# Three-chunk first task and a position-major last projection in a two-layer encoder

## The chip, the core and the metric

The kernel runs on one core of a Trainium2 chip. The metric is device time in microseconds. In the profile PE is TensorE (PEld its weight loads), DVE is VectorE, ACT is ScalarE, POOL is GpSimd and SP is the queue that issues most DMAs.

## The reference

Two layers of a pre-norm encoder on x of 512 positions and 1024 features, all float32. Each layer projects the normed x once, feeds two attention branches, multiplies each by a SiLU gate, and projects back with a residual add. A norm ends the whole.

```python
for layer in range(DEPTH):                       # DEPTH = 2
    h = rms_norm(x, norm_g[layer])
    p = h @ w_in[layer]                          # 1024 -> 6304
    c_q, c_kv, k_r, gate_a, dil_qkv, gate_b = jnp.split(p, split_points, axis=-1)
    a = mla_attention(c_q, c_kv, k_r, ...) * jax.nn.silu(gate_a)     # 8 heads, low-rank q (384) and kv (256)
    b = dilated_attention(dil_qkv, cos_d, sin_d) * jax.nn.silu(gate_b)  # 3 groups x 8 heads
    x = x + jnp.concatenate([a, b], axis=-1) @ w_out[layer]          # 1024 -> 1024
return rms_norm(x, final_g)
```

## The kernel before, in words

**Precision.** Every operand of a large product is held as two parts, hi and lo. `triple` issues three matmuls per product: hi by hi, hi by lo, lo by hi. Weights come from HBM as tiles of 128 x 512 (`wst`, in the order of `PLAN`). `prefetch` loads a tile into `wraw` (3 buffers), ScalarE converts the hi part (L192) and VectorE subtracts for the lo part (L197); the result lies in `whl` (4 buffers). `weight` asks for tiles three ahead of the one in use. `hl` (14 buffers of hi and lo, 128 x 512) holds the normed input chunks, the latents and the eight chunks that the output projection reads.

**Layout.** Features lie on the partitions and positions along the free axis: x is eight chunks of 128 features x 512 positions. `take_x` multiplies a chunk by the norm's gain and splits it (L270 on ScalarE, L271 on VectorE). The norm's factor per position is applied later, so products start before it is known. `add_square` squares a chunk and adds it to a running sum `L.ss` on GpSimd (L265); `norm` turns the sum to positions with transposes (L250).

**Order.** `Weave` writes the order of the program out ahead of time: a main list of tasks (projections) advances a clock by the cost that each step yields, and side lists (norms, scores, values, combinations) step in where their needs are done and a lag has passed. The instructions of an engine run in the order that results after the compiler's scheduling.

**The start.** Eight x chunks are loaded on SP's queue with the first four weight tiles among them, `take_x` is issued for each and then all squares, the first two of them on GpSimd. The first main task, ("ckv",), is `latent_pair`: for each x chunk, six matmuls into two banks. Then comes ("v", 1, 0), the value projection of 288 columns, and then ("cq", 2), ("cq", 0), ("cq", 1), 24 matmuls each. `keep_latent` stores a result and adds its square (L347, GpSimd).

**The end of a layer.** The output projection has eight blocks n of 128 output features, each a sum over eight chunks `ms`: four from the first branch (`mo`) and four from the second (`do`). `out_part` runs some chunks of one block: tasks "wp" (chunks 0 to 3), "wq" (4 and 5, as soon as do 0 and 1 are there) and "wo" (the rest). Before the last ones the second branch's unit 11 has to be finished: transposes, value products (`far_out`, L766), `combine`, `combine_last`. `out_add` loads the x chunk into `xl` (2 buffers), adds it to the bank (L829), and in layer 0 stores it to `x1d` and hands it to the next layer's `take_x` and `add_square`.

**The end of the kernel.** In layer 1 the blocks 3, 4, 6 and 7 are computed in two halves of 256 positions (`out_halves`), so that `final` can start on the first half. `out_add` squares each result on ScalarE (L832), multiplies it by the final gain (L833) and adds squares on GpSimd (L839). `final` turns the sums (L250), forms the factor with small VectorE instructions (L890 to L899), spreads it by transposes (L904) and multiplies each block (L913 for the first half, L915 for the second) before eight stores.

Of the kernel before, what the change touches and what calls it, by code (L numbers as in the profile page):

```python
# [7 lines left out]
F32 = mybir.dt.float32  # L8
# [6 lines left out]
S = 512  # L15
# [22 lines left out]
def plan():  # L38

    t = []  # L40
    for task in ORDER:
        n = {"v": 8 if task == ("v", 1, 0) else 4, "mv": 1, "muk": 1, "mur": 1, "muq": 1 - task[1] % 2 if len(task) > 1 else 0, "kr": 0}.get(task[0], 2)
        t += [("ckv", c, i) for i in range(2) for c in range(2)] if task[0] == "ckv" else [task + (i,) for i in range(n)]
    t += [("wo", n, 0) for n in range(5)] + [("wo", n, 1) for n in range(3)]
    t += [("wo", n, i) for n, i in ((5, 0), (3, 1), (4, 1), (5, 1), (6, 0), (6, 1), (7, 0), (7, 1))]
    return t
# [3 lines left out]
PLAN = plan()  # L50
ADDED = ("dqk", "nv", "ga", "gb")
FIRST = PLAN.index(("dqk", 0, 1, 1))
# [79 lines left out]
def hybrid_encoder(ctx, tc, xT, wst, gains, tables, keytab, masks, out):  # L132
# [36 lines left out]
    gn = const.tile([128, 2 * NG + 8], F32, name="gn")  # L169
# [14 lines left out]
    def prefetch(upto):  # L184
        while emitted[0] < min(upto, len(queue)):
            l, i = queue[emitted[0]]
            c = WCOLS.get(PLAN[i][0] if PLAN[i][:3] != ("v", 1, 0) else "vk", 512)
            raw = t([128, 512], F32, "wraw", 3)
            nc.sync.dma_start(raw[:, :c], wst[l * len(PLAN) + i, :, :c])
            w = wtile(l, PLAN[i])  # L190
            hi, lo, src = w[:, 0, :c], w[:, 1, :c], raw[:, :c]
            nc.scalar.copy(hi, src)  # L192
            if PLAN[i][0] in ADDED and i > FIRST:
# [4 lines left out]
            ready[(l,) + PLAN[i]] = w  # L198
# [57 lines left out]
    def add_square(L, x, pool=False):  # L256
        q = tmp()
        if pool:
            nc.gpsimd.tensor_tensor(q, x, x, op=ALU.mult)
        else:  # L260
            nc.scalar.activation(q, x, AF.Square)
        if L.ss is None:
            L.ss = q
        else:
            nc.gpsimd.tensor_tensor(L.ss, L.ss, q, op=ALU.add)  # L265
# [16 lines left out]
    Z = Layer()  # L282
    Z.ss, Z.q = None, []

    nc.scalar.activation(ones[:, 1:2], ones[:, 0:1], AF.Exp)
    warm = hl()
# [4 lines left out]
    xs = []  # L291
    for k in range(8):
        x = ogt() if k < 6 else xl()
        nc.sync.dma_start(x, xT[128 * k:128 * k + 128])
        xs.append(x)
        take_x(layers[0], k, x)
        if k in (0, 4):
            prefetch(emitted[0] + 2)
    for k, x in enumerate(xs):
        add_square(layers[0], x, k < 2)  # L300
# [32 lines left out]
    def keep_latent(L, name, c, a):  # L333
# [12 lines left out]
        else:  # L346
            nc.gpsimd.tensor_tensor(L.sq[name], L.sq[name], q, op=ALU.add)  # L347
# [7 lines left out]
    def latent_pair(L):  # L355

        a = [bank(), bank()]
        for i in range(2):
            w = [weight(L.l, "ckv", c, i) for c in range(2)]
            for k in range(4 * i, 4 * i + 4):  # L360
                for c in range(2):
                    quads(a[c], w[c], L.h[k:k + 1], k, 8)
                if k < 7:
                    yield 1.3, 0.0
        for c in range(2):
            keep_latent(L, "ckv", c, a[c])
        yield 1.3, 0.0
# [454 lines left out]
    def out_add(L, n, a, c, last):  # L822

        if n not in L.x:
            x = ogt() if last and n in (3, 4) else xl()
            nc.sync.dma_start(x, (xT if L.l == 0 else x1d)[128 * n:128 * n + 128])
            L.x[n] = (x, ogt() if last and n in (0, 1, 2, 5) else x)
        x, y = L.x[n]
        nc.vector.tensor_tensor(y[:, c], x[:, c], a, op=ALU.add)  # L829
        if last:  # L830
            q = tmp()
            nc.scalar.activation(q[:, c], y[:, c], AF.Square)  # L832
            nc.scalar.mul(y[:, c], y[:, c], gn[:, 2 * NG + n:2 * NG + n + 1])  # L833
            if n == 0:
                Z.ss = q
            elif n > 5:
# [281 lines left out]
```

## Time and profile before

| | |
|---|---|
| median of 3 runs | 949.06 us (949.03 to 950.31) |
| profiled execution | 949.16 us |
| its span | 947.4 us |
| PE busy | 913.3 us (96%) |
| VectorE busy | 698.8 us (74%) |
| ScalarE busy | 599.7 us (63%) |
| GpSimd busy | 342.5 us (36%) |
| HBM read, written | 112.74 MB, 4.36 MB |

A row of the order of time gives start, length, engine, source line, operation, output and input with shapes, count, and in brackets the idle time of the engine ahead of it with what ended it. L235 to L237 are the three matmuls of `triple`. A matmul's length is its latency; what one costs in a stream is the step from one start to the next.

### The profile page before, as it was taken

What the parts mean: (1) busy time and instruction counts of PE and PEld (TensorE: products, weight loads), DVE (VectorE), ACT (ScalarE), POOL (GpSimd) and SP (SyncE); (2) the same over time, 40 slices, a digit from 0 to 9 for tenths busy, and PEclk for the clock granted to TensorE, in tenths of its full rate; (3) what the DMA queues carried; (4) which work ended last, traced back from release to release, by engine and by line L of the source; (5) the groups of instructions that cost most, each with busy time, mean ns of one, the idle gap of its engine ahead of it and who ended that gap; (6) DMA issues with size and microseconds to landing.
All of it is one profiled execution on the core that took longest, in us unless ns stands there. A gap on an engine that the chain in (4) does not pass through costs nothing.

```text
span 947.4 us, 16052 instructions
## 1 busy us (share of the span) xinstructions
PE 913.3 (96%) x5252; PEld 777.3 (82%) x5252; DVE 698.8 (74%) x1730; ACT 599.7 (63%) x1447; POOL 342.5 (36%) x393
## 2 busy tenths in 40 slices
PE   7999999999999999998999999999999989999995
PEld 4978888988889889877897888888888878887874
DVE  7756788967868766787766488797876866857775
ACT  5546786666857766754554578666766666676452
POOL 6125262344632431333211435424554224234223
PEclk9999999999999999999999999999999999999997
DMA  6448443177553764652653754516756455376342
GB/s 228 132 109 170 105 101 87 48 163 157 117 127 90 147 133 101 140 139 90 217 167 97 167 118 91 109 43 144 145 124 136 112 118 111 92 149 142 99 135 90
DMA packets 83123, 118.15 MB, mean 125 GB/s; under 512 B 16800, under 2 KB 31968, under 8 KB 83040
## 3 DMA queue, kind: packets, MB, share of 16 engines
q1 hardware_dynamic: 63456, 81.47, 29.7%
q0 software_dynamic: 19584, 35.66, 23.8%
q8 instruction: 41, 0.67, 0.3%
q14 instruction: 42, 0.34, 0.1%
HBM read 112.74 MB, written 4.36 MB: 124 GB/s over the span
## 4 chain that ended last, share of the span: by engine, by line
PE 78%; DVE 9%; ACT 4%; DMA 3%; issue 3%; POOL 1%; SPq 1%; DVEq 0%; POOLq 0%; ACTq 0%
PE bank L235 22%; PE bank L236 21%; PE bank L237 21%; PE bank L430 4%; PE bank L531 3%; PE bank L725 1%; DMA whl<-wst 1%; PE bank L654 1%; PE bank L766 1%; DVE pt L216 1%; DMA tmp<-shd 1%; DVE whl L197 1%; ACT p L509 1%; DVE tmp L611 1%; ACT whl L192 1%
## 5 line engine op out<-in xcount | busy, mean ns | idle before, releaser
L235 PE MATMUL bank<-hl,whl 128*128 128x512 f32 (+1 forms) x836 | 329.8, 396 | 7.1 <-ACT hl L215 4.8
L237 PE MATMUL bank<-hl,whl 128*128 128x512 f32 (+1 forms) x836 | 324.2, 388 | 5.3 <-DMA whl<-wst 3.4
L236 PE MATMUL bank<-hl,whl 128*128 128x512 f32 (+1 forms) x836 | 325.1, 389 | 1.8 <-DVE hl L271 1.7
L192 ACT CAST whl<-wraw 128x512 fp32r<-128x512 f32 (+2 forms) x256 | 151.5, 597 | 123.7 <-PE bank L237 83.9
L195 POOL DMA_DIRECT2D whl<-wst x136 | 119.8, 890 | 222.9 <-ACT whl L194 154.5
L237 PEld LDWEIGHTS bank<-hl,whl 128*128 128x128 f32 x836 | 157.6, 189 | 40.0 <-DMA whl<-wst 4.2
L235 PEld LDWEIGHTS bank<-hl,whl 128*128 128x128 f32 x836 | 157.4, 189 | 39.3 <-ACT hl L215 6.3
L236 PEld LDWEIGHTS bank<-hl,whl 128*128 128x128 f32 x836 | 158.0, 189 | 31.9 <-DVE hl L271 4.0
L197 DVE TENSOR_TENSOR whl<-wraw,whl 128x512 fp32r<-128x512 f32 (+3 forms) x120 | 87.9, 741 | 37.1 <-ACT whl L192 35.7
L609 POOL TENSOR_TENSOR tmp<-tmp,sd 128x512 f32<-128x512 f32 x48 | 63.1, 1315 | 88.7 <-DVE tmp L607 72.0
L216 DVE TENSOR_TENSOR pt<-bank,pt 128x512 fp32r<-128x512 f32 x128 | 83.6, 683 | 5.4 <-ACT pt L215 4.0
L194 ACT ACTIVATE whl<-wraw 128x512 fp32r<-128x512 f32 x136 | 86.3, 634 | 0.1
L235 PE MATMUL bank<-whl,hl 128*128 128x256 f32 (+1 forms) x288 | 83.1, 290 | 0.0
L236 PE MATMUL bank<-whl,hl 128*128 128x256 f32 (+1 forms) x288 | 82.1, 285 | 0.0
L237 PE MATMUL bank<-whl,hl 128*128 128x256 f32 (+1 forms) x288 | 82.0, 285 | 0.0
L215 ACT CAST pt<-bank 128x512 fp32r<-128x512 f32 x128 | 69.8, 588 | 10.0 <-PE bank L430 9.6
L511 POOL TENSOR_SCALAR p<-p,lc 128x512 f32<-128x512 f32 x64 | 48.7, 768 | 73.6 <-DVE lc L510 72.8
L430 PE MATMUL bank<-ident,p 128*128 128x128 f32 x512 | 67.0, 273 | 0.0
L430 PEld LDWEIGHTS bank<-ident,p 128*128 128x128 f32 x512 | 58.6, 140 | 5.4
L738 ACT ACTIVATE p<-p,st 128x128 f32<-128x128 f32 x128 | 50.0, 393 | 15.1 <-DVE st L734 14.8
L509 ACT ACTIVATE p<-bank,nm 128x512 f32<-128x512 f32 x64 | 43.5, 684 | 23.3 <-DVE nm L506 22.9
L235 PEld LDWEIGHTS bank<-whl,hl 128*128 128x128 f32 x288 | 54.7, 190 | 0.6
(183 smaller groups left out, 1566.6 us busy)
## 6 DMA issues: line engine op xcount, KB each, us to landing
wraw<-wst SPq DMA_DIRECT2D x224, 256.0 KB, 3.1
whl<-wst POOLq DMA_DIRECT2D x136, 256.0 KB, 4.5
tmp<-shd SPq DMA_DIRECT2D x32, 128.0 KB, 3.3
xl<-xT SPq DMA_DIRECT2D x10, 256.0 KB, 2.6
wraw<-wst SPq DMA_DIRECT2D x16, 144.0 KB, 2.9
wraw<-wst SPq DMA_DIRECT2D x12, 192.0 KB, 2.4
x1d<-xl SPq DMA_DIRECT2D x8, 256.0 KB, 2.3
out_dram<-p SPq DMA_DIRECT2D x8, 256.0 KB, 2.1
```

The lines of the kernel that those rows point to most:

```text
L192: nc.scalar.copy(hi, src)
L194: nc.scalar.mul(lo, src, -1.0)
L195: nc.gpsimd.dma_start(lo, wst[l * len(PLAN) + i, :, :c], accum_op=ALU.add)
L197: nc.vector.tensor_tensor(lo, src, F(hi), op=ALU.subtract)
L215: nc.scalar.copy(dst_hi, src)
L216: nc.vector.tensor_tensor(dst_lo, src, F(dst_hi), op=ALU.subtract)
L235: nc.tensor.matmul(a, w[:, 0], h[:, 0], start=first, stop=False)
L236: nc.tensor.matmul(a, w[:, 0], h[:, 1], start=False, stop=False)
L237: nc.tensor.matmul(a, w[:, 1], h[:, 0], start=False, stop=last)
L430: nc.tensor.transpose(b[:, 128 * i:128 * i + 128], x, ident)
L509: nc.scalar.activation(pt, s, AF.Exp, bias=nm[:, qb, a:a + 1], scale=1.0, accum_out=l1)
L609: nc.gpsimd.tensor_tensor(u, u, L.sd, op=ALU.mult)
```

## The change

1. *First task.* In layer 0, ("ckv",) and ("cq", 2) become one task of three chunks (`latent_first`): nine matmuls for each x chunk. Its six weight tiles are loaded into `p` tiles and held in `hl`. The first 128 columns of three tiles are loaded as pieces on ScalarE's DMA queue; the rest comes on SP's queue behind the second x chunk and the fifth.
2. *Squares.* In layer 0 all squares are formed on ScalarE inside the first task and added on VectorE. In both layers the ("ckv") square is added on VectorE.
3. *Layer 0's output.* The tasks "wq" run for five blocks instead of three, and the second-half weight tiles of blocks 0 to 4 lie in `hl`.
4. *Layer 1's output.* Positions lie on the partitions: four blocks sc of 128 positions, two halves of 512 features. The residual block is loaded from `x1d` in a rearranged form, transposed into the bank, and the products are added onto it; weight tiles are 128 x 512 slices of one chunk each. `out_sums` squares the bank with a sum per partition on ScalarE, forms the factor with nine small VectorE instructions, multiplies by factor and gain (a broadcast tile `L.gb`) and stores 128 x 512 pieces. `out_halves`, `final` and the last sums on GpSimd are gone.

```diff
+    one, rest = slice(0, 128), slice(128, 512)
+    raws = [t([128, 512], F32, "p", 8) for _ in range(6)]
...
+    for j in range(3):
+        nc.scalar.dma_start(raws[j][:, one], wst[j, :, one])
...
     for k in range(8):
...
+        load(k)
+        if k == 1:
+            for j in range(3):
+                nc.sync.dma_start(raws[j][:, rest], wst[j, :, rest])
+        elif k == 4:
+            for j in range(3, 6):
+                nc.sync.dma_start(raws[j], wst[j])
+    for j in range(3):
+        take_weights(j, one)
+    for k in range(8):
+        take_x(layers[0], k, xs[k])
+        if k in (1, 4):
+            for j in range(3):
+                take_weights(j if k == 1 else j + 3, rest if k == 1 else slice(0, 512))
...
+    def latent_first(L):
+
+        chunks = FIRST if L.l == 0 else FIRST[:2]
+        a = [bank() for _ in chunks]
         for i in range(2):
-            w = [weight(L.l, "ckv", c, i) for c in range(2)]
+            w = [weight(L.l, *c, i) for c in chunks]
             for k in range(4 * i, 4 * i + 4):
-                for c in range(2):
+                for c in range(len(chunks)):
                     quads(a[c], w[c], L.h[k:k + 1], k, 8)
+                if L.l == 0:
+                    add_square(L, xs[k])
...
-            nc.gpsimd.tensor_tensor(L.ss, L.ss, q, op=ALU.add)
+            (nc.gpsimd if L.l else nc.vector).tensor_tensor(L.ss, L.ss, q, op=ALU.add)
...
-            nc.gpsimd.tensor_tensor(L.sq[name], L.sq[name], q, op=ALU.add)
+            (nc.vector if name == "ckv" else nc.gpsimd).tensor_tensor(L.sq[name], L.sq[name], q, op=ALU.add)
...
-        if l + 1 == DEPTH and key[0] == "wo" and key[1] > 5:
+        if key[0] == "wo" and (key[1] < 6 and key[2] if l + 1 == DEPTH else key[1] < 5 and key[2]):
             return hl()
...
+    def load_x(L):
+
+        sc, half = L.order.pop(0)
+        x = xl()
+        nc.sync.dma_start(x.rearrange("p (n c) -> p n c", n=4),
+                          x1d[512 * half:512 * half + 512, 128 * sc:128 * sc + 128].rearrange("(n p) c -> p n c", p=128))
+        L.x.append(x)
...
+    def out_rows(L, blocks, half, chunks):
 
         ms = L.mo + L.do
...
+        for sc in blocks:
+            if (sc, half) not in L.acc:
+                a, x = bank(), L.x.pop(0)
+                for j in range(4):
+                    nc.tensor.matmul(a[:, 128 * j:128 * j + 128], x[:, 128 * j:128 * j + 128], ident, start=j == 0, stop=False, is_transpose=True)
+                L.acc[sc, half] = a
+                if L.order:
+                    load_x(L)
+                yield 0.44, 0.0
+        for k in chunks:
+            if (k, half) not in L.wo:
+                L.wo[k, half] = weight(L.l, "wo", k, half)
+            for sc in blocks:
+                triple(L.acc[sc, half], ms[k][:, :, 128 * sc:128 * sc + 128], L.wo[k, half], False, k == 7)
+                if k == 7:
+                    out_sums(L, sc, half)
+                yield 0.65, 0.0
+
+    def out_sums(L, sc, half):
...
+        a = L.acc[sc, half]
+        if half == 0:
+            L.o[sc] = [t([128, S], F32, "p", 8) for _ in range(2)], sm(2, "sq%d" % sc)
+        o, ss = L.o[sc]
+        nc.scalar.activation(tmp(), a, AF.Square, accum_out=ss[:, half:half + 1])
+        if half == 0:
+            nc.vector.tensor_tensor(o[0], a, L.gb[:, 0], op=ALU.mult)
+            return
...
+        nc.scalar.mul(o[0], o[0], r)
+        nc.vector.scalar_tensor_tensor(o[1], a, r, L.gb[:, 1], op0=ALU.mult, op1=ALU.mult)
+        for j in (1, 0):
+            nc.sync.dma_start(out[128 * sc:128 * sc + 128, 512 * j:512 * j + 512], o[j])
...
+            task(main, k("wa"), now(*mla), out_rows, (0, 1), 0, range(4))
+            task(main, k("wb"), [], out_rows, (2,), 0, range(4))
+            task(main, k("wc"), now(k("s", "d", 11)), out_rows, (3,), 0, range(4))
+            task(main, k("wd"), [], out_rows, (0,), 1, range(4))
+            task(main, k("we"), now(*early), out_rows, range(4), 0, (4, 5))
+            task(main, k("wf"), [], out_rows, (0,), 1, (4, 5))
+            task(main, k("wg"), now(k("o", "d", 11)), out_rows, (1,), 1, range(6))
+            task(main, k("wh"), now(*late), out_rows, range(4), 0, (6, 7))
+            task(main, k("wi"), [], out_rows, (0, 1), 1, (6, 7))
+            for sc in (2, 3):
+                task(main, k("wj", sc), [], out_rows, (sc,), 1, range(8))
+            continue
...
-        for n in range(3):
+        for n in range(5):
             task(main, k("wq", n), now(*early), out_part, n, range(4, 6))
```

More of the change, by code (lines that the diff above doesn't have):

```diff
@@ L129, in run, with hybrid_encoder @@
                 return
-def hybrid_encoder(ctx, tc, xT, wst, gains, tables, keytab, masks, out):
+def hybrid_encoder(ctx, tc, xT, wst, gains, fgain, tables, keytab, masks, out):
     nc = tc.nc
@@ L820, in combine_last, with out_add @@
         yield 0.0, 0.5
[L822 to L836, printed above, removed]
-                Z.q.append(q[:, c])
-            else:
-                nc.gpsimd.tensor_tensor(Z.ss[:, c], Z.ss[:, c], q[:, c], op=ALU.add)
-            return
-        nc.sync.dma_start(x1d[128 * n:128 * n + 128], y)
-        take_x(layers[L.l + 1], n, y)
-        add_square(layers[L.l + 1], y)
+    def out_add(L, n, a):
+        x = xl()
+        nc.sync.dma_start(x, xT[128 * n:128 * n + 128])
+        nc.vector.tensor_tensor(x, x, a, op=ALU.add)
+        nc.sync.dma_start(x1d[128 * n:128 * n + 128], x)
+        take_x(layers[L.l + 1], n, x)
+        add_square(layers[L.l + 1], x)
     def out_part(L, n, chunks):
@@ L894, in final @@
         nc.vector.tensor_scalar(h, m, -0.5, 0.0, op0=ALU.mult, op1=ALU.add)
         for _ in range(3):
-            for i in range(2):
-                yi = y[:, i:i + 1]
-                nc.vector.scalar_tensor_tensor(z[:, i:i + 1], yi, yi, h[:, i:i + 1], op0=ALU.mult, op1=ALU.mult)
-            nc.vector.scalar_tensor_tensor(y, z, 1.5, y, op0=ALU.add, op1=ALU.mult)
-        rst = y
-        yield 0.6, 2.5
-        b = bank()[:, 0:256]
-        for i in range(2):
-            nc.tensor.transpose(b[:, 128 * i:128 * i + 128], rst[:, i:i + 1].to_broadcast([128, 128]), ident)
@@ L985, in hybrid_encoder @@
         last = l + 1 == DEPTH
+        if last:
+            at = [i for i, x in enumerate(main) if x[0] == k("gb", 2)][0]
+            line = []
+            task(line, k("ahead"), now(k("mur", 1)), load_ahead)
+            main[at:at] = line
+            task(main, k("wa"), now(*mla), out_rows, (0, 1), 0, range(4))
[9 more added lines that the diff above has]
+                task(main, k("wj", sc), [], out_rows, (sc,), 1, range(8))
+            continue
@@ L986, in hybrid_encoder @@
         for n in range(3):
             task(main, k("wp", n), now(*mla), out_part, n, range(4))
-        if last:
-            task(main, k("wp", 3), now(k("s", "d", 11)), out_halves, (3, 4), range(4), range(2))
-        else:
-            for n in (3, 4):
-                task(main, k("wp", n), now(k("s", "d", 11)), out_part, n, range(4))
-        for n in range(3):
+        for n in (3, 4):
+            task(main, k("wp", n), now(k("s", "d", 11)), out_part, n, range(4))
+        for n in range(5):
@@ L1115 @@
     out = np.empty((S, D), np.float32)
-    out[order()] = r.results[0]["out_0_dram"].T
+    out[order()] = r.results[0]["out_0_dram"]
     return out[None]
```

156 lines of the change are left out of this document (61 added, 95 removed).

## The prediction, on record before the result

> **What bounds the kernel now.** I read the page first, then the busy time by stretches, then the order of time at both ends and at the two output projections.
>
> ```profile
> span 947.4 us, 16052 instructions
> PE 913.3 (96%) x5252; PEld 777.3 (82%) x5252; DVE 698.8 (74%) x1730; ACT 599.7 (63%) x1447; POOL 342.5 (36%) x393
> PE 78%; DVE 9%; ACT 4%; DMA 3%; issue 3%; POOL 1%; SPq 1%; DVEq 0%; POOLq 0%; ACTq 0%
> ```
>
> TensorE is busy for 96% of the span and is 78% of the chain that ended last. So a change pays where TensorE stands still, or where its work disappears. The stretches (length, busy time of PE, weight loads, VectorE, ScalarE, GpSimd, then granted clock, DMA share, GB/s) show where it stands:
>
> ```profile
> 15.00:20.00 5.00, 2.14 (x7) 1.18 (x7) 5.00 (x4) 1.60 (x4) 4.76 (x4) 0.97 0.34 88
> 20.00:25.00 5.00, 5.00 (x17) 3.91 (x16) 2.24 (x3) 0.31 (x1) 0.66 (x1) 0.69 0.51 161
> 38.90:56.00 17.10, 17.10 (x81) 14.17 (x80) 12.37 (x34) 8.85 (x20) 2.79 (x5) 1.00 0.32 96
> 880.00:890.00 10.00, 8.71 (x39) 6.71 (x38) 9.28 (x28) 5.33 (x17) 4.19 (x6) 1.00 0.21 60
> 900.00:910.00 10.00, 8.41 (x43) 6.59 (x42) 9.42 (x18) 3.17 (x7) 1.64 (x1) 1.00 0.19 58
> 910.00:920.00 10.00, 9.47 (x55) 7.99 (x54) 7.13 (x10) 7.54 (x13) 2.59 (x2) 1.00 0.55 162
> 935.00:948.00 13.00, 1.57 (x9) 0.73 (x7) 7.36 (x26) 0.93 (x2) 3.36 (x5) 0.61 0.47 161
> ```
>
> From 15 to 20 us VectorE is full (5.00 of 5.00) and TensorE at 2.14; then the granted clock drops to 0.69. In the last 13 us TensorE has 1.57 us of work. Between these ends little is lost.
>
> **The start, part by part.** Three things change: the columns for chunk 0 come first as small pieces through ScalarE's queue; the running sum of squares leaves GpSimd; and the first task takes ("cq", 2) along, so each x chunk feeds nine matmuls instead of six.
>
> ```profile
> 4.04 0.72 ACT L270 ACTIVATE hl<-og,gn 128x512 fp32r<-128x512 f32 x1 [1.80 <-DMA og<-xT]
> 4.72 0.62 ACT L192 CAST whl<-wraw 128x512 fp32r<-128x512 f32 x1
> 4.79 0.82 DVE L271 SCALAR_TENSOR_TENSOR hl<-og,gn,hl 128x512 fp32r<-128x512 f32 x1 [3.35 <-ACT hl L270]
> 5.53 0.68 DVE L197 TENSOR_TENSOR whl<-wraw,whl 128x512 fp32r<-128x512 f32 x1
> 8.10 6.38 DVE L271 SCALAR_TENSOR_TENSOR hl<-og,gn,hl 128x512 fp32r<-128x512 f32 x4 [0.17 <-ACT hl L270]
> 8.90 5.02 POOL L265 TENSOR_TENSOR tmp<-tmp,tmp 128x512 f32<-128x512 f32 x3
> 25.17 0.55 PE L235 MATMUL bank<-whl,hl 128*128 128x288 f32 x3
> 38.69 0.60 PE L250 MATMUL bank<-ident,tmp 128*128 128x128 f32 x4
> 39.04 0.47 PE L235 MATMUL bank<-hl,whl 128*128 128x512 f32 x1
> 39.35 0.39 PE L236 MATMUL bank<-hl,whl 128*128 128x512 f32 x1
> 45.74 0.39 PE L237 MATMUL bank<-hl,whl 128*128 128x512 f32 x1
> 59.79 0.66 PE L250 MATMUL bank<-ident,tmp 128*128 128x128 f32 x4 [0.95 <-POOL tmp L347]
> GB/s 0 0 23 161 391 259 199 303 328 344 393 404 404 385 385 386 383 400 373 188 18 0 23 174 0 193 309 358 36 35 251 154 106 0 0 0 201 266 230 55
> wraw<-wst SPq DMA_DIRECT2D x4, 256.0 KB, 5.8
> ```
>
> *Why VectorE is late now.* The residual-part instruction of take_x took 0.82 us at 4.79 and 6.38/4 = 1.60 us each while GpSimd added squares beside it. With those seven adds on VectorE nothing runs on GpSimd there; they cost 7 x 0.68 = 4.8 us of VectorE, but stand behind all take_x work in order.
>
> *TensorE's need.* From 39.35 to 45.74 lie 28 steps of a 512-wide matmul: 6.39/28 = 0.228 us. The first task becomes 72 x 0.228 = 16.4 us, and the 24 matmuls of ("cq", 2), 24 x 0.228 = 5.5 us, vanish behind the value task. So today the equivalent point is 25.17 + 5.5 = 30.7 us.
>
> *When it is fed.* The throughput row (40 slices of 0.75 us over the first 30 us) adds up to 0.47 MB (gains, three 64 KB pieces, the first x) at about 4.0 us; with half a microsecond to land, 4.5. ScalarE now also issues three DMAs ahead of its table load, but its first conversion is at 4.04 today. 0.72 of ScalarE and 0.82 of VectorE give the second half at 6.1, and eight more matmuls end chunk 0 at 8.0. The rest of the three pieces (1.32 MB in all) is through at 7.2 and landed near 8, just in time; its conversions are 3 x 0.5 on ScalarE and 3 x 0.55 on VectorE (from 0.62 and 0.68, scaled for 384 columns). The last x (3.7 MB in all) lands near 14, and its VectorE part is done by 16, while TensorE comes to it at 8.0 + 6 x 2.05 = 20.3. So from chunk 1 TensorE is the limit: 8.0 + 63 x 0.228 = 22.4, and 0.5 for hand-overs: 22.9 us instead of 30.7, **-7.8 us**. Bounds: as early as now (5.4 + 16.4 = 21.8) gives -8.9; the same 25.17 as now gives -5.5. I take the inner value because it is counted from rows of this very stretch.
>
> *Is it kept?* The six weight tiles sit in hl and p, so whl and wraw are free for the value task's first weights. SP's queue has the same x loads and tables; the fourth weight no longer waits there for a free raw buffer. In the 17.10 us of the three cq chunks VectorE works 12.37; without ("cq", 2) TensorE has 11.6 us there and VectorE 12.37 - 2 x 0.68 - 0.82 = 10.2. It still fits, narrowly. The ("ckv") add on VectorE costs and gains nothing: the wait for L347 at 59.79 is for the cq sum, which stays on GpSimd.
>
> **Layer 0's output.** Chunks 4 and 5 of n = 3, 4 move ahead of the second half of unit 11, with the second-half weights in hl instead of the four whl.
>
> ```profile
> PE bank L235 <- ACT hl L215: 1.3, 1, 1.3
> PE bank L766 <- DVE pt L216: 0.2, 1, 0.2
> L829 DVE TENSOR_TENSOR xl<-xl,bank x8: 676/686/691, 451.5 to 477.6; 128x512 f32<-128x512 f32 x8
> 479.07 0.75 DVE L271 SCALAR_TENSOR_TENSOR hl<-xl,gn,hl 128x512 fp32r<-128x512 f32 x1 [0.79 <-ACT hl L270]
> 480.37 0.39 PE L235 MATMUL bank<-hl,whl 128*128 128x512 f32 x1
> ```
>
> The waits of 440 to 450 us are 1.5 us; 12 x 0.228 = 2.7 us of moved work covers them. But the last value products of unit 11 then stand about 0.9 us later, and the eight residual adds (two xl buffers, 26.1 us from first to last) start from there. Today the last chunk is ready at 479.82, 0.55 us before its use; that slack goes and most of the 1.5 is waited again: **-0.4**, between -1.5 and +1.5.
>
> **The last projection.** Same products: 4 position blocks x 2 halves x 8 chunks x 3 = 192 of 512 columns; today 96 of these are pairs of 256.
>
> ```profile
> 919.44 0.28 PE L235 MATMUL bank<-hl,hl 128*128 128x256 f32 x1
> 925.08 0.28 PE L237 MATMUL bank<-hl,hl 128*128 128x256 f32 x1
> xl<-xT SPq DMA_DIRECT2D x10, 256.0 KB, 2.6
> tmp<-shd SPq DMA_DIRECT2D x32, 128.0 KB, 3.3
> ```
>
> 47 steps in 5.64 us: 0.12 for 256 columns, so full width saves 96 x (0.24 - 0.228) = 1.1 us. New are 32 transposes that put the residual into PSUM; four took 0.35 (38.69 to 39.04): +2.8. The 8 transposes of the first half's final norm go: -0.7. In the planner's order 27 matmuls (6 today) now stand between unit 11's transposes and its value products, and a transposed block with 18 (12 today) between these and the late chunks; there TensorE idles 1.59 + 0.53 = 2.1 us from 900 to 920: -2.1. Sum **-1.1**; if the idle time stays and the halves cost nothing, +2.1; if the transposes also fill the 1.3 us idle of 880 to 890, -2.4. VectorE loses eight residual adds and gains four multiplications and 36 tiny ones, ScalarE loses eight gain products and gains four, GpSimd is freed: all beside 40 us of matmuls. A new wait stands in SP's queue: the third residual block waits for a transpose to free one of two buffers, with weight loads behind it; these run three tiles ahead. The gain's 512 KB load waits for the rope tile's last reader, long done.
>
> **The tail.** Now: last matmul at 934.75, end at 947.4, 12.65 us.
>
> ```profile
> 934.75 0.29 PE L237 MATMUL bank<-hl,hl 128*128 128x256 f32 x1
> 938.87 0.16 DVE L899 SCALAR_TENSOR_TENSOR sfy<-sfz,sfy 128x2 f32<-128x2 f32 x1
> 940.02 0.16 DVE L899 SCALAR_TENSOR_TENSOR sfy<-sfz,sfy 128x2 f32<-128x2 f32 x1
> 943.02 0.74 DVE L915 TENSOR_TENSOR p<-xl,bank 128x256 f32<-128x256 f32 x2
> out_dram<-p SPq DMA_DIRECT2D x8, 256.0 KB, 2.1
> L509 ACT ACTIVATE p<-bank,nm 128x512 f32<-128x512 f32 x64 | 43.5, 684 | 23.3 <-DVE nm L506 22.9
> 878.09 0.19 ACT L738 ACTIVATION_READ_ACCUMULATOR p<-p,st 128x1 f32 x1
> ```
>
> After: matmul and hand-over 0.34; square with sum, like the exponential from PSUM, 0.68 + 0.19; hand-over 0.1; nine tiny VectorE instructions at 1.15/6 = 0.19 (six steps lie between 938.87 and 940.02) = 1.73; the product out of PSUM 0.82, with ScalarE's 0.72 beside it; then what now follows the last VectorE instruction (943.76 to 947.4), 3.64, and 0.4 as two stores come together: 7.9 with a hand-over. **-4.7**; -5.2 without the second store, -3.5 if two stores take turns and each hand-over costs 0.3 more.
>
> **Sum.** -7.8 - 0.4 - 1.1 - 4.7 = -14.0: span 933.4. The profiled execution took 949.16, 1.76 beyond its span, and the median of the runs is 949.06, so the forecast is 935.2 us, 14.0 under the profiled execution and 13.9 under the median. All bounds together: -18.0 to -5.4.
>
> **Rivals.**
> (a) *The clock drops at the new start too.* For it: the clock fell after a stretch in which TensorE was busy 2.14 of 5 us. Against: there is less idle time now between 5 and 8 us. Price: 0.31 of 5 us, 1.6; 936.8. Chance 0.10. The Trainium skill, "TensorE: Matmul & The Clock Gate", What's actually happening, has the clock fall after a whole idle window of some 3.4 us and warm again after one busy window. By that rule the new start keeps full clock and the sum stays; the trace does not quite agree, since its fall came with 2.14 us of matmuls in the five before.
> (b) *VectorE takes over behind the value task.* 10.2 us of partly dependent work in 11.6: if it needs its old pace for half of the removed 5.5, 2.7 come back: 937.9. Chance 0.14.
> (c) *More is filled*: chunk 0 as early as now (-1.1), layer 0's wait gone (-1.1), transposes free in 880 to 890 (-1.3): 931.7. Chance 0.13.
> (d) *Slower: the residual loads bind.* A block is now 512 rows of 512 bytes. With two buffers a load is hidden while it lands within about 6 us (two blocks of 12 x 0.228 + 0.35); to lose 14.0 over six further loads, each must cost 2.3 more of TensorE's time, landing after some 11 us: 950. A 256 KB load lands in 2.6, and 128 KB in such short rows in 3.3; twice that is 6.6. Chance 0.04.
> (e) *The shorter ends do not matter*, the time staying within 0.2%: the chain passes through both ends, so only 0.02.
>
> **Numbers.** The forecast itself has 0.57, with its own range 932.3 to 938.2. (a) and (b) are slower, (c) faster, and all but (d) and (e) are well below 949; 0.2% (1.9 us) is about what a measurement tells from no change. Range 930.5 to 941.2: it leaves out (d), (e) and the far corners. Faster 0.94, same 0.02, slower 0.04.
>
> **What would show it.** The 288-column matmuls begin near 22.9 us, with the VectorE part of take_x at 0.8 us each; granted clock 1.0 from 15 to 25; the three latent chunks' end 7.8 us earlier; no wait on hl between the two halves of unit 11; 32 transposes at 0.09 us; under 8 us between the last matmul and the end. Wrong it would be by a late start of the value task, a wait of TensorE for x's last chunk at the layer boundary, or weight casts that stall ahead of the last projection.

## The result and the profile after

The changed kernel takes 933.06 us, the median of four runs (932.15 to 936.2); before, 949.04 (946.65 to 950.31). The ratio is 0.984 (95% interval 0.981 to 0.9871): shorter by 16 us, 1.6 per cent. The forecast was 935.2 with a range of 930.5 to 941.2. The profiled execution is the longest of the four: 936.2 us, of which the span is 934.4, 13.0 below the span before.

Of the page, the same three lines as before:

```profile
span 934.4 us, 15835 instructions
PE 910.4 (97%) x5172; PEld 775.1 (83%) x5172; DVE 690.9 (74%) x1732; ACT 597.8 (64%) x1448; POOL 315.1 (34%) x367
PE 81%; DVE 8%; ACT 4%; DMA 3%; issue 3%; POOL 1%; ACTq 0%; DVEq 0%; POOLq 0%
```

TensorE has 2.9 us less busy time, and the span is 13.0 shorter: most of the gain is time in which it stood still. The busy time by stretches (columns as before: PE, weight loads, VectorE, ScalarE, GpSimd, granted clock, DMA share, GB/s):

```profile
15.00:20.00 5.00, 5.00 (x24) 4.14 (x23) 4.79 (x9) 3.95 (x9) 0.00 (x0) 1.00 0.72 249
20.00:25.00 5.00, 5.00 (x25) 4.18 (x24) 1.29 (x3) 1.45 (x3) 0.00 (x0) 1.00 0.48 144
880.00:890.00 10.00, 10.00 (x45) 8.12 (x46) 8.26 (x16) 4.28 (x10) 3.87 (x6) 0.83 0.54 165
927.00:934.40 7.40, 0.42 (x2) 0.00 (x0) 2.32 (x10) 1.41 (x3) 0.00 (x0) 0.80 0.20 78
```

From 15 to 25 us TensorE is now full at full clock (it was at 2.14 of 5.00, then at 0.69). From 880 to 890 the clock fell to 0.83, which it had not before. The last stretch without matmuls is 7.4 us.

**Where the 13.0 us came from.** The trace gives it by landmarks that both kernels have: the sums of squares that end the three latent chunks (csq), a gate at the end of layer 0's second branch, the first values of layer 1 (kraw), the first product with layer 1's last `mo` chunk, the last matmul. Rows in the order of time, before and then after:

```profile
67.76 0.60 ACT L382 ACTIVATE csq<-bank 128x512 f32<-128x512 f32 x1 [0.30 <-PE bank L230]
426.27 0.63 ACT L406 ACTIVATE gate<-tmp 128x512 f32<-128x512 f32 x1 [1.32 <-DVE tmp L414]
494.39 0.28 ACT L581 ACTIVATE kraw<-bank,rst 128x32 f32<-128x32 f32 x1
888.05 0.73 PE L235 MATMUL bank<-hl,whl 128*128 128x512 f32 x2 [1.29 <-ACT hl L215]
```

```profile
61.75 0.60 ACT L409 ACTIVATE csq<-bank 128x512 f32<-128x512 f32 x1 [0.26 <-PE bank L237]
421.58 0.63 ACT L433 ACTIVATE gate<-tmp 128x512 f32<-128x512 f32 x1 [1.33 <-DVE tmp L441]
488.22 0.28 ACT L608 ACTIVATE kraw<-bank,rst 128x32 f32<-128x32 f32 x1
878.94 0.50 PE L242 MATMUL bank<-whl,hl 128*128 128x512 f32 x1 [1.54 <-ACT hl L222]
927.03 0.39 PE L244 MATMUL bank<-whl,hl 128*128 128x512 f32 x1
```

| stretch | before | after | difference | forecast |
|---|---|---|---|---|
| start to csq | 67.76 | 61.75 | -6.0 | -7.8 |
| csq to gate | 358.51 | 359.83 | +1.3 | 0 |
| gate to kraw (layer 0's output) | 68.12 | 66.64 | -1.5 | -0.4 |
| kraw to last `mo` | 393.66 | 390.72 | -2.9 | 0 |
| last `mo` to last matmul | 46.70 | 48.09 | +1.4 | -1.1 |
| last matmul to end | 12.65 | 7.37 | -5.3 | -4.7 |
| sum | 947.4 | 934.4 | -13.0 | -14.0 |

The second stretch holds no edit. The fourth holds none but at its end, since the new order reaches the last `mo` chunk with other work done: ahead of it stand 25 of the projection's matmuls before, and 18 of them, eight transposes and four more value products after. At 0.228, 0.1 and 0.116 us a piece that moves 0.3 us of work from the fourth row into the fifth. Like for like the two are nearer to -2.5 and +1.1; their sum, -1.5, stays. The rest of the differences in the second and fourth stretch goes with two things that vary from run to run: the granted clock (first row after, second before) and a wait for a weight load (before, then after).

```profile
134.00:155.00 21.00, 20.55 (x114) 17.44 (x113) 15.04 (x44) 13.32 (x36) 6.31 (x8) 0.92 0.47 90
770.00:860.00 90.00, 87.29 (x530) 74.77 (x529) 58.38 (x168) 58.79 (x154) 27.74 (x29) 0.98 0.60 127
777.56 0.79 PE L237 MATMUL bank<-hl,whl 128*128 128x512 f32 x1 [2.71 <-DMA whl<-wst]
770.00 0.50 PE L244 MATMUL bank<-hl,whl 128*128 128x512 f32 x1 [1.39 <-DMA whl<-wst]
```

0.08 of 21 us is 1.7; 0.02 of 90 is 1.8, and the wait is 1.3 shorter. The clock record of each trace has one stretch of half rate there, 3.41 us long (from 136.18 us after, from 777.49 before). In the profiles of the experiments csq to gate takes 357.6 to 359.6 us with the same instructions. So effects of under 2 us are read below from the stretch that holds them, not from whole times.

**The start after the change.** In order of time:

```profile
1.49 3.78 PE L303 MATMUL bank<-q 128*128 128x512 f32 x8 [1.49 <-DVE q L300]
3.55 0.28 ACT L222 CAST hl<-p 128x128 fp32r<-128x128 f32 x1
4.51 0.30 ACT L222 CAST hl<-p 128x128 fp32r<-128x128 f32 x1 [0.68 <-DMA p<-wst]
5.77 0.30 ACT L222 CAST hl<-p 128x128 fp32r<-128x128 f32 x1 [0.97 <-DMA p<-wst]
5.98 1.33 ACT L274 ACTIVATE hl<-og,gn 128x512 fp32r<-128x512 f32 x2
6.75 1.65 PE L242 MATMUL bank<-hl,hl 128*128 128x512 f32 x3 [1.47 <-ACT hl L274]
8.62 0.63 PE L244 MATMUL bank<-hl,hl 128*128 128x512 f32 x1
9.05 0.63 PE L243 MATMUL bank<-hl,hl 128*128 128x512 f32 x1
15.32 0.74 DVE L275 SCALAR_TENSOR_TENSOR hl<-og,gn,hl 128x512 fp32r<-128x512 f32 x1
24.68 0.29 PE L242 MATMUL bank<-whl,hl 128*128 128x288 f32 x1
```

The three pieces land one after another, ScalarE waits for the second and the third, and the first x chunk's conversion, which follows them in ScalarE's order, begins at 5.98. TensorE stands still for 1.47 us, and then steps by 0.43 us (8.62 to 9.05) instead of 0.228 until 9.90: half rate. It had not been any faster before that: the eight dummy matmuls ahead (first row) take 3.78 us and step by 0.43 too. The clock record of the trace begins only at 9.89, with full clock; the 1.00 that a window shows for the time before means that the record has no entry there. VectorE's part of `take_x` is at 0.74 us, undisturbed.

**The last projection and the tail after the change.**

```profile
882.23 0.63 PE L242 MATMUL bank<-whl,hl 128*128 128x512 f32 x1
882.65 0.63 PE L243 MATMUL bank<-whl,hl 128*128 128x512 f32 x1
904.30 0.47 PE L793 MATMUL bank<-pt,v 128*128 128x256 f32 x2 [1.51 <-DVE og L799]
927.52 0.60 ACT L919 ACTIVATE tmp<-bank 128x512 f32<-128x512 f32 x1 [2.62 <-PE bank L244]
928.24 0.21 DVE L925 TENSOR_SCALAR smsy<-smsq 128x1 f32<-128x1 f32 x1 [3.24 <-ACT tmp L919]
930.15 0.75 DVE L932 SCALAR_TENSOR_TENSOR p<-bank,smsy,mr 128x512 f32<-128x512 f32 x1
```

Half rate again at 882 (in the clock record from 880.29 to 883.70), a new wait of 1.51 us before the second half of unit 11's value products, and then the tail as the forecast described it: square, nine tiny instructions from 928.24, the product, the stores.

### The profile page after: what moved, and what is told of

It is laid out like the page before. It is cut to its first block, busy times and chain, and to the rows that moved or that the text cites. A ratio compares the mean times of both kernels' runs of the same rounds, so it can differ in the third digit from the quotient of the medians.

```text
span 934.4 us, 15835 instructions
## 1 busy us (share of the span) xinstructions
PE 910.4 (97%) x5172; PEld 775.1 (83%) x5172; DVE 690.9 (74%) x1732; ACT 597.8 (64%) x1448; POOL 315.1 (34%) x367
## 4 chain that ended last, share of the span: by engine, by line
PE 81%; DVE 8%; ACT 4%; DMA 3%; issue 3%; POOL 1%; ACTq 0%; DVEq 0%; POOLq 0%
PE bank L242 22%; PE bank L244 22%; PE bank L243 22%; PE bank L457 5%; PE bank L558 3%; PE bank L752 1%; PE bank L793 1%; PE bank L681 1%; DMA whl<-wst 1%; DVE pt L223 1%; DMA wraw<-wst 1%; ACT whl L199 1%; DVE tmp L638 1%; POOL tmp L636 1%; DVE whl L204 1%
## 5 line engine op out<-in xcount | busy, mean ns | idle before, releaser
L242 PE MATMUL bank<-hl,whl 128*128 128x512 f32 x728 | 290.2, 399 | 2.2 <-ACT hl L222 1.4
L244 PE MATMUL bank<-hl,whl 128*128 128x512 f32 x728 | 284.4, 391 | 2.0 <-DMA whl<-wst 2.0
L243 PE MATMUL bank<-hl,whl 128*128 128x512 f32 x728 | 284.5, 391 | 0.0
L199 ACT CAST whl<-wraw 128x512 fp32r<-128x512 f32 (+3 forms) x243 | 143.8, 596 | 119.4 <-PE bank L244 77.5
L244 PEld LDWEIGHTS bank<-hl,whl 128*128 128x128 f32 x728 | 136.7, 188 | 32.5 <-DMA whl<-wst 2.9
L242 PEld LDWEIGHTS bank<-hl,whl 128*128 128x128 f32 x728 | 136.6, 188 | 29.2 <-ACT hl L222 1.8
L243 PEld LDWEIGHTS bank<-hl,whl 128*128 128x128 f32 x728 | 137.0, 188 | 24.6 <-DVE hl L223 0.3
L242 PE MATMUL bank<-whl,hl 128*128 128x256 f32 (+2 forms) x328 | 99.8, 304 | 1.5 <-ACT hl L222 1.5
L244 PE MATMUL bank<-whl,hl 128*128 128x256 f32 (+2 forms) x328 | 98.3, 300 | 0.0
L243 PE MATMUL bank<-whl,hl 128*128 128x256 f32 (+2 forms) x328 | 98.1, 299 | 0.0
L204 DVE TENSOR_TENSOR whl<-wraw,whl 128x512 fp32r<-128x512 f32 (+3 forms) x107 | 76.1, 717 | 26.0 <-ACT whl L199 25.0
L242 PEld LDWEIGHTS bank<-whl,hl 128*128 128x128 f32 x328 | 62.5, 191 | 3.9 <-ACT hl L222 1.8
L244 PEld LDWEIGHTS bank<-whl,hl 128*128 128x128 f32 x328 | 62.5, 191 | 2.0 <-DVE hl L223 0.4
L243 PEld LDWEIGHTS bank<-whl,hl 128*128 128x128 f32 x328 | 62.5, 191 | 1.7
```

The lines of the kernel that those rows point to most:

```text
L204: nc.vector.tensor_tensor(lo, src, F(hi), op=ALU.subtract)
L242: nc.tensor.matmul(a, w[:, 0], h[:, 0], start=first, stop=False)
L243: nc.tensor.matmul(a, w[:, 0], h[:, 1], start=False, stop=False)
L244: nc.tensor.matmul(a, w[:, 1], h[:, 0], start=False, stop=last)
```

## The experiments

All kernels of one group ran on one chip beside the kernel before. Medians over four to six runs each. The changed kernel itself ran beside group 1 only, so groups 2 and 3 are compared with it by their stretches, not by their times.

**Group 1: the parts** (before: 948.95 us, 946.6 to 954.0).

*The changed kernel again.* No edit.

> The changed kernel once more, as the yardstick for the other three. Theory of additive parts: the profiled execution (936.2) was an unlucky one; half-rate stretches of TensorE (6.75 to 9.7 us and 880.2 to 883.6 us, about 1.4 us each) come and go, so the median is 932.5 to 934 and the profiles differ in such stretches, not in the order of work. Rival: 936 is the rule on this profile's chip, and the stretches are in every profile.

935.55 us (933.05 to 936.99), ratio 0.9846 (0.9813 to 0.9879). That is above the 932.5 to 934 of the theory and close to the rival's 936. Its profile, span 932.3, has half rate at the start, from the first product at 6.40 until 10.83, and none in the last projection, so the second of the two stretches is not in every profile:

```profile
8.27 0.63 PE L244 MATMUL bank<-hl,hl 128*128 128x512 f32 x1
8.70 0.63 PE L243 MATMUL bank<-hl,hl 128*128 128x512 f32 x1
879.00 0.50 PE L242 MATMUL bank<-whl,hl 128*128 128x512 f32 x1 [1.55 <-ACT hl L222]
902.18 0.47 PE L793 MATMUL bank<-pt,v 128*128 128x256 f32 x2 [0.88 <-DVE og L799]
924.93 0.39 PE L244 MATMUL bank<-whl,hl 128*128 128x512 f32 x1
```

From the last `mo` to the last matmul it takes 924.93 - 879.00 = 45.93 us, 0.8 *less* than before: the +1.4 of the first profile is not the change's price.

*The start alone.* The two output projections as before.

Cut from its difference to the kernel before:

```diff
-        if pool:
-            nc.gpsimd.tensor_tensor(q, x, x, op=ALU.mult)
-        else:
-            nc.scalar.activation(q, x, AF.Square)
+        nc.scalar.activation(q, x, AF.Square)
...
-                task(main, k(*o), [], *((latent_chunk, "cq", a[0]) if a else (latent_pair,)))
+                task(main, k(*o), [], *((nothing,) if l == 0 and o in FIRST else (latent_chunk, "cq", a[0]) if a else (latent_first,)))
```

> The new start (pieces, three chunks, VectorE adds) with both output projections as before. Theory of additive parts: -6.0 us as at the end of the third latent chunk in the changed kernel's trace (67.76 to 61.75), so 943 us. Rival (VectorE or the weight stream takes the gain back behind the value task, case (b) of the prediction): 945 to 949.

942.79 us (939.5 to 945.79), ratio 0.992 (0.989 to 0.995): -6.2, as the theory had it. Start to csq is 62.17 us, -5.6.

*Layer 1's projection alone.* Start and layer 0 as before. Cut from its difference to the changed kernel:

```diff
-                task(main, k(*o), [], *((nothing,) if l == 0 and o in FIRST else (latent_chunk, "cq", a[0]) if a else (latent_first,)))
+                task(main, k(*o), [], *((latent_chunk, "cq", a[0]) if a else (latent_pair,)))
...
-        for n in range(5):
+        for n in range(3):
             task(main, k("wq", n), now(*early), out_part, n, range(4, 6))
```

> Only layer 1's projection with positions on the partitions; start and layer 0 as before. Theory of additive parts: tail -5.3 (12.65 to 7.37 us from the last matmul's start to the end), stretch from the last wait on hl to the last matmul -1.1 to +1.4, so 943 to 945.5 us. Rival (the projection gains only the tail and the transposes cost 2.8 more than forecast): 946.5 or more.

940.86 us (940.05 to 944.87), ratio 0.9909 (0.9881 to 0.9937): -8.1. That is below the theory's 943 to 945.5: the edit is worth more than the expected 3.9 to 6.4, and where the surplus comes from was not traced. The profiled execution, the slowest of its runs, gives -6.6 from kraw to the end. Its start, with the same code as before, reaches csq 1.5 us later (69.27), with half rate from 19.05 to 25.88 instead of 19.73 to 23.15. Start and projection alone add up to -14.3, the whole came to -13.4 in the same group; with layer 0's part (next) the parts exceed the whole by 2 to 3 us, so at the scatter of these medians additive parts are not refuted, and not shown to the microsecond.

*The change without layer 0's part.* "wq" for three blocks, second-half weights in `whl`.

```diff
-        for n in range(5):
+        for n in range(3):
             task(main, k("wq", n), now(*early), out_part, n, range(4, 6))
...
-        if key[0] == "wo" and (key[1] < 6 and key[2] if l + 1 == DEPTH else key[1] < 5 and key[2]):
+        if key[0] == "wo" and l + 1 == DEPTH and key[1] < 6 and key[2]:
```

> The changed kernel with layer 0's output as before (wq for three blocks, second-half weights in the four whl buffers). Theory: the idle of 1.5 us between 440 and 450 us comes back and nothing else, so 1.5 us above the changed kernel, about 934.6. Rival (what the prediction held): the last x chunk's slack of 0.55 us ate most of the gain, so 0.4 above the changed kernel, 933.5, with TensorE waiting for the last chunk at the layer boundary in the changed kernel's trace.

936.69 us (932.01 to 940.09), ratio 0.9855 (0.9822 to 0.9887), 1.1 above the repeat: by the time alone nothing could be said. The stretch can say it. First what TensorE waits for between 412 and 488 us in the changed kernel, then without this part (engine, tile, line, releaser; us in total, times, longest):

```profile
PE bank L242 <- ACT hl L222: 1.4, 1, 1.4
PE bank L793 <- DVE og L799: 0.4, 1, 0.4
```

```profile
PE bank L242 <- ACT hl L222: 2.6, 2, 1.4
PE bank L793 <- DVE pt L223: 0.2, 1, 0.2
420.51 0.63 ACT L433 ACTIVATE gate<-tmp 128x512 f32<-128x512 f32 x1 [1.33 <-DVE tmp L441]
488.57 0.28 ACT L608 ACTIVATE kraw<-bank,rst 128x32 f32<-128x32 f32 x1
```

One of two waits of 1.3 for late chunks goes, and gate to kraw takes 68.06 us without this part, 66.64 with it. In all profiles of this study the four kernels without it lie at 68.06 to 68.21 and the ten with it at 66.29 to 66.86. The two groups do not touch: the part is worth 1.2 to 1.9 us.

**Group 2: what the start's gain is made of** (before: 947.25 us, 944.76 to 956.12).

*The squares' adds back on GpSimd.*

```diff
-            (nc.gpsimd if L.l else nc.vector).tensor_tensor(L.ss, L.ss, q, op=ALU.add)
+            nc.gpsimd.tensor_tensor(L.ss, L.ss, q, op=ALU.add)
```

> The changed kernel with layer 0's squares added on GpSimd again. Theory: GpSimd beside VectorE stretches take_x's VectorE part from 0.74 to about 1.6 us as in the kernel before, so the last of eight is late for TensorE by the third to eighth chunk; TensorE waits on hl in the first 25 us and the value task starts 1 to 3 us later than at 24.68: 935 to 938. Rival (the pieces and the third chunk alone give the start its gain, VectorE's adds none): within 1 us of the changed kernel, value task at 24.7, VectorE stretched but not waited for.

934.08 us (932.02 to 937.57), ratio 0.9847 (0.9808 to 0.9886). The time is below the theory's 935. In the trace the stretching came back, and part of the loss with it:

```profile
12.43 4.10 DVE L223 TENSOR_TENSOR hl<-p,hl 128x512 fp32r<-128x512 f32 x3
16.45 1.78 DVE L275 SCALAR_TENSOR_TENSOR hl<-og,gn,hl 128x512 fp32r<-128x512 f32 x1
18.28 0.50 PE L243 MATMUL bank<-hl,hl 128*128 128x512 f32 x1 [0.86 <-DVE hl L275]
61.38 0.60 ACT L409 ACTIVATE csq<-bank 128x512 f32<-128x512 f32 x1 [0.27 <-PE bank L237]
```

VectorE needs 1.78 instead of 0.74 us for a `take_x` part while GpSimd adds beside it, and TensorE waits 0.86 us once: the two steps around that wait (17.03 to 18.62) take 1.59 us instead of 0.46, so the stretching costs about 1.1. That the value task still begins at 24.31, ahead of the changed kernel's 24.68, is luck of the clock: here it had risen at 5.32, ahead of the first product at 6.42, and no half rate came. So with nine matmuls to a chunk (2.05 us) VectorE's pace is almost enough, and its undisturbed adds are worth about 1 us, the lower end of what was expected.

*Two chunks in the first task*, with early pieces and VectorE's adds.

```diff
-        chunks = FIRST if L.l == 0 else FIRST[:2]
+        chunks = FIRST[:2]
```

> The changed kernel with the first task of two chunks; (cq, 2) goes back behind the value task; pieces and VectorE adds stay (two pieces instead of three, four whole tiles instead of six). Theory (pieces and undisturbed VectorE feed TensorE faster than even six matmuls per chunk use up): first task ends near 18.6 to 19 us, the same work done 0 to 1 us earlier than in the changed kernel: 933 to 935. Rival (the third chunk is what covers the arrival of x): TensorE waits for x chunks and the time is 3 to 5 us above the changed kernel, 937 to 940.

932.56 us (931.03 to 933.9), ratio 0.9826 (0.9788 to 0.9863); csq at 60.72, 1.0 earlier than in the changed kernel, so the rival (3 to 5 us later) is out: no wait of TensorE between the first product and the value task (18.12) ends with VectorE. Whether the third chunk brings nothing is not shown by this, because two things favour the pair here. Only two pieces are waited for, so that the first product begins at 5.63 instead of 6.75, and the clock rose at 7.26 instead of 9.89. Together that is worth about 1.8 us, of which 1.0 is left at csq.

*Twelve dummy matmuls instead of eight* at the start, against the half rate.

```diff
-STEP, LD0, WARM, LG2, LY = 2, 10.0, 8, 16.5, 5.0
+STEP, LD0, WARM, LG2, LY = 2, 10.0, 12, 16.5, 5.0
```

> The changed kernel with 12 instead of 8 matmuls ahead of the first x chunk. Theory (TensorE falls to half rate because it stands idle between 5 us and the first x): the steps of 0.43 us between 6.4 and 10.6 us go, which are 1.0 to 1.6 us, so 932 to 933.5. Rival (the half rate has nothing to do with that gap, or the longer run of dummies delays the first chunk): steps of 0.43 us stay or the first real matmul starts after 7.0; within 0.5 us of the changed kernel.

933.22 us (931.06 to 934.7), ratio 0.9833 (0.9795 to 0.9871). The clock rose at 5.80 in this profile, during the dummies, and no product ran at half rate. The other part of the rival came too: x was converted at 6.39 and the first product begins at 7.17, after 7.0. Even so the value task begins at 23.95, 0.7 earlier than in the changed kernel, and csq is at 61.02.

*The three first pieces packed into one array*, so that one load brings 128 rows of 1536 bytes instead of three loads of 128 rows of 512.

```diff
-    for j in range(3):
-        nc.scalar.dma_start(raws[j][:, one], wst[j, :, one])
+    nc.scalar.dma_start(first, wone)
```

> The three first pieces come as one load of 128 x 384 with rows of 1536 bytes from an array of their own, instead of three loads with rows of 512 bytes. Theory (the short rows on ScalarE's queue hold up the first x chunk, which lands at 5.6 to 6.2 us instead of 4.0): the first x chunk is converted by 5.0 instead of 5.6 to 6.2 and the value task starts 0.7 to 1.5 us earlier: 932 to 934. Rival (x's landing is set by the bytes ahead of it and the second chunk behind, not by row length): the same within 0.3 us.

931.51 us (930.3 to 931.83), ratio 0.9814 (0.9773 to 0.9854). No run of it is as long as the shortest of the kernel with GpSimd's adds on the same chip.

```profile
3.25 0.70 ACT L222 CAST hl<-p 128x128 fp32r<-128x128 f32 x3 [0.57 <-DMA p<-wone]
3.96 0.72 ACT L274 ACTIVATE hl<-og,gn 128x512 fp32r<-128x512 f32 x1
5.05 0.85 PE L242 MATMUL bank<-hl,hl 128*128 128x512 f32 x3
22.16 0.29 PE L242 MATMUL bank<-whl,hl 128*128 128x288 f32 x1
59.21 0.60 ACT L409 ACTIVATE csq<-bank 128x512 f32<-128x512 f32 x1 [0.26 <-PE bank L237]
875.88 0.50 PE L242 MATMUL bank<-whl,hl 128*128 128x512 f32 x1 [1.53 <-ACT hl L222]
921.42 0.39 PE L244 MATMUL bank<-whl,hl 128*128 128x512 f32 x1
```

The first conversion of x is 2.0 us earlier than in the changed kernel, the first matmul 1.7, the value task 2.5, csq 2.5: more than the theory's 0.7 to 1.5. The clock had part in that, since it rose at 4.99 here and no product ran at half rate. The same bytes were loaded, so the late pieces held up the start, not the throughput of the queues. Whether the shorter rows or the three loads in turn made them late was not separated.

**Group 3: the new wait, and combinations** (before: 949.99 us, 945.84 to 955.19).

*One accumulator fewer held.* Block 0 of the second half moves behind unit 11's value products.

```diff
-            task(main, k("wd"), [], out_rows, (0,), 1, range(4))
...
-            task(main, k("wf"), [], out_rows, (0,), 1, (4, 5))
-            task(main, k("wg"), now(k("o", "d", 11)), out_rows, (1,), 1, range(6))
+            task(main, k("wg"), now(k("o", "d", 11)), out_rows, (0, 1), 1, range(6))
```

The order of the weight tiles follows.

> The changed kernel with one accumulator fewer held early in the last projection: the tasks "wd" and "wf" (block 0 of the second half, chunks 0 to 5) move into "wg", behind unit 11's value products, and the weight tiles are reordered to match. Nothing is left out. Theory: the 1.51 us for which TensorE stands still before the second pair of unit 11's value products (waiting for VectorE's merge of the first pair, L799) is a wait for a PSUM bank, since five accumulators are held there. With four held that wait falls below 0.3 us, the span falls by 1 to 1.5 us, and the time comes out at 931.5 to 934.5. Rival: the second pair waits for what the first pair's merge makes in any case; the wait stays at about 1.5. Second rival: the 18 matmuls moved away (18 x 0.228 = 4.1 us) were the cover for unit 11's operands; TensorE then stands still before the first value products (L793 on pt) by 1 us or more, and the time is that of the changed kernel or later.

936.86 us (932.35 to 938.48), ratio 0.9843 (0.9814 to 0.9873). The second rival held:

```profile
895.76 2.04 PE L793 MATMUL bank<-pt,v 128*128 128x256 f32 x8 [2.52 <-DVE pt L223]
898.43 1.94 PE L897 MATMUL bank<-ident,xl 128*128 128x128 f32 x8 [0.64 <-ACT tmp L796]
```

The eight value products now run in one go, so the wait between them was for a bank, as the theory had it. But the 18 matmuls taken away were the cover for their operands: TensorE stands still 2.52 us before them, and the stretch from the last `mo` (878.30) to the last matmul (929.32) grew to 51.02 us. Of that growth 3.4 is the clock: after the wait the record has half rate from 895.83 to 902.65. The last run below has the same order without it.

*Packed pieces with two chunks.* The edits of both.

> Two edits that each came out slightly ahead, together: a first task of two chunks instead of three, and the first columns of its two weight tiles as one 128 x 256 load with rows of 1024 bytes. Nothing is left out. Theory (TensorE is the limit once the first x chunk is there, and the third chunk brings nothing): the first matmul at 5.0 to 5.3 instead of 6.75, the value task as much earlier than the pair's 18.12 as the first matmul is earlier than its 5.63, at 17.3 to 17.9, sums at the end of the three latent chunks near 59 to 60.2; time 930.5 to 932.5. Rival (VectorE feeds the pair, and an earlier first chunk does not help six matmuls per chunk): value task at 18.1 or later, latent chunks' end at 60.7 and the time at 932.5 or more.

933.03 us (932.66 to 934.93), ratio 0.9817 (0.9789 to 0.9845). First matmul at 5.07, value task at 17.84 (18.12 without packing), csq at 60.52. The value task lies in the theory's range, the time in the rival's, csq between the two. The first product came only 0.6 earlier than without packing (5.63), and 0.3 of that reached the value task. From the first product to the value task the pair takes 12.77 us for 48 matmuls, which at 0.228 are 10.9: the rest is half rate until 5.86, slow steps from 6.6 to 7.6, one wait of 0.29 for VectorE at 9.49 and one of 0.33 for the value task's weight. So the rival's VectorE is only a small part of it. With packing the third chunk pays: csq at 59.21 with it, 60.52 with the pair.

*Packed pieces with twelve dummies.* The edits of both.

> Packed first pieces (one load with rows of 1536 bytes) and twelve dummy matmuls ahead of the first chunk instead of eight. Nothing is left out. Theory: with the first x at about 4.0 there is no half-rate step at the start with eight dummies already, so four more bring nothing: first matmul 5.0, value task 22.2, latent chunks' end 59.2, and a time within 0.2% of the packed kernel's 931.5. Rival (the dummies themselves delay): first real matmul at 5.5 or later and a time above 932.

932.03 us (931.01 to 933.62), ratio 0.9804 (0.9776 to 0.9833). The rival held, the dummies now delay: all twelve ran at half rate (the clock rose at 6.73), x is converted at 3.96, but the first matmul begins at 6.76, and csq stands at 60.18, 1.0 later than packed with eight.

*Packed pieces with the later accumulator.* The edits of both.

> Packed first pieces together with the later accumulator ("wd" and "wf" inside "wg"). Nothing is left out. Theory: the two gains lie 840 us apart and add: packed 931.5 less 1.0 to 1.5, so 930.0 to 930.5, span 927.5 to 928.5. Rival (the bank wait was replaced by another of equal size): 931.5 as the packed kernel alone; if the cover was lost, 932 to 933.

933.65 us (931.21 to 940.23), ratio 0.9828 (0.9795 to 0.9861). The gains did not add, since the later accumulator is no gain: the stretch from the last `mo` to the last matmul is 48.43 us, 2.9 more than packed alone (45.54), with no half rate in it. TensorE waits there for 2.1 us ahead of the value products and for 1.1 ahead of the transposes that follow them; so the cover was lost.

## Why the prediction was right, step by step

**The bound and the sum.** TensorE as the limit, with gains only where it stands still, was right. The sum of -14.0 met -13.0 in the first profile and -15.1 in the repeat (span 932.3). The terms came out unevenly, and that the total came so close is in part luck: the start gave 1.8 less than forecast, layer 0 and the tail together 1.7 more, and each stretch of half rate that comes or goes moves a profile by 1.7.

**The start: -7.8 forecast, -6.0 measured, -5.5 to -5.8 in the four others with the same start.** Two steps of the sum failed. One is "with half a microsecond to land, 4.5". It took the throughput of all queues together and let every load in the sum be there at that time; in fact the pieces came one by one until 5.77, and ScalarE's order put x behind them. x was converted at 5.98 instead of 4.5, 1.5 later. For the half microsecond of landing in that step no row was given. The other is "eight more matmuls end chunk 0 at 8.0", which took full rate for granted; eight steps at 0.43 instead of 0.228 would cost 1.6. Chunk 0 ended at 10.36 in the changed kernel. From there the sum held: 63 x 0.228 = 14.4 more is 24.7, the value task came at 24.68, and the 0.5 for hand-overs was not needed. With both out of the way, packed, the value task began at 22.16 (22.9 forecast) and csq came 8.5 earlier (67.76 - 59.21), within the bounds of -8.9 to -5.5.

Two edits were made against the late VectorE. The runs showed that undisturbed adds alone remove it as the limit (six matmuls to a chunk: no wait of TensorE that ends with VectorE), and nine matmuls alone all but about 1.1 us of it (adds on GpSimd). The forecast gave both credit together. The kernel with neither, but with early pieces, was not tried.

Rival (b), VectorE behind the value task, did not come: from the value task to csq are 61.75 - 24.68 = 37.1 us, before 67.76 - 25.17 = 42.6, so the whole 5.5 us of ("cq", 2) were kept.

Rival (a), a slower clock at the start, came in another way than it was told. With one exception the clock did not drop there: it had not risen yet. In all fourteen profiles TensorE begins at half rate, and the clock record begins with the rise, between 4.95 and 10.86 us. It rose last, at 9.89 to 10.86, in the four profiles where the idle time ahead of the first product (1.12 to 1.74 us) lay before the rise; in the others it had risen by 7.26. The exception is the run with the later accumulator: full clock from 4.95, then 1.82 us of idle time, and half rate from 8.36 to 11.77. Half rate was priced at 1.6; in the repeat ten steps from 6.40 to 10.83 cost 4.43 - 10 x 0.228 = 2.2. So the chance of 0.10 was too small: products ran at half rate in all five profiles with this start. The argument "there is less idle time now between 5 and 8 us" was wrong twice: there was more (1.47 us against 0.62), and the clock had first to rise. Later in the program length alone does not decide either: after the idle time of 1.5 us at 878 the clock fell in three profiles of this study and stayed in nine. The Trainium skill, "TensorE: Matmul & The Clock Gate", What's actually happening, has a window of some 3.4 us that runs freely, so that the moment of a change varies between runs of one kernel; the coming and going here agrees. So do the stretches of half rate in the clock records, which last 3.41 us or twice that while matmuls run. That the clock falls only after a whole idle window of some 3.4 us does not agree with the fall at 880.29 here, ahead of which TensorE had stood still for 1.54 us only.

**Layer 0's output: -0.4 forecast, -1.5 measured**, the lower bound. The step "that slack goes and most of the 1.5 is waited again" was wrong: in the changed kernel TensorE waits for nothing at the boundary. One wait of 1.3 for the second half's chunks is gone, and nothing replaced it.

**The last projection: -1.1 forecast, +1.4 in the first profile.** The terms themselves held: in the seven profiles with this order and full clock there the stretch takes 45.3 to 45.9 us, -0.8 to -1.4 against 46.70, and 0.3 more is gained in the stretch ahead, as said under the table. One profile is not much to measure against, but a second agrees: the run with the start alone has the old projection too, and its 48.75 us less 1.7 of half rate (from 897.95) are 47.0. The first profile lost 1.7 us to the clock (0.83 for 10 us) and 1.51 to a wait that the forecast had not named: the second half of unit 11's value products waits for a bank, since accumulators are held in the others. At full clock that wait is 0.2 to 0.9. So "there TensorE idles 2.1 us: -2.1" was too hopeful by up to 0.9, and the rest of the sum made up for it. The residual loads (rival d) never show as a wait of TensorE.

**The tail: -4.7 forecast, -5.3 measured**, 7.37 us for 7.9; between 7.36 and 7.59 in every other profile with it. The nine tiny instructions and their hand-over take 1.84 us (928.24 to 930.08; 1.73 forecast). From the end of the product (930.15 + 0.75) to the end of the span are 3.5 us, not 3.64 + 0.4: the second store added nothing that shows.

**What was not in the sum.** The stretch without an edit differs by +1.3 us between the two profiles, the one from kraw to the last `mo` by -2.9, of which only 0.3 is the edit's, so the median's 2.1 us below the forecast, and the repeat's 0.35 above it, are not evidence on any single term.

## What to carry to other kernels

When a sum of bytes says that loads are there, ask for each load in which order its consumer's engine takes it: a small late piece ahead of a large early one, in the same engine's order, delays both. Two cures for one limit need not add, so try each alone; the second may become useful only when the next limit is moved, as the third chunk did with packed pieces. Before two starts are compared, look when the clock rose in each: a difference of 1 to 2 us can be that alone. Where a kernel's whole time scatters by several microseconds, compare the stretch between two landmarks around the edit: 1.5 us that no whole time could show stood clear there.

## What was not expected of the hardware

Three loads of 64 KB in rows of 512 bytes were ready by 3.5, at 4.5 and at 5.8 us; the same 192 KB as one load in rows of 1536 bytes was ready at 3.25. The Trainium skill, "DMA: Bandwidth & Descriptors", Specifications, puts the least transfer for full rate at 512 bytes; here rows of that size, in three loads beside another queue's, came 2.5 us later.

TensorE began every one of the fourteen executions at half rate (steps of 0.43 us instead of 0.228 for 512 columns), dummies included, and went to full rate between 4.95 and 10.86 us. The clock record has no entry before the rise, so a window over that time shows 1.00 while matmuls run at half rate. An idle time of 1.1 to 1.7 us between the dummies and the first product went with the latest rises.

Two stores of 256 KB issued together ended 3.5 us after the last product; the last store before the change ended after 3.64.
